# Gate and up of both feed-forward blocks from seven half-size products, with pieces of the down projection between them

## The chip, the cores and the metric

One Trainium2 chip; the kernel runs on one of its cores. The metric is the device time of one execution in microseconds (us), from the first to the last instruction on that core with what the runtime puts around it; less is better. TensorE (PE) does the matmuls, VectorE (DVE), ScalarE (ACT) and GpSimd (POOL) the elementwise work, and one queue, SP, issues all transfers (DMA).

## The reference, cut to what matters

A two-layer decoder trunk over 512 tokens of 1024 features in float32: an attention mixer, an output projection and a SwiGLU feed-forward block (FFN) in each layer. The change concerns the two FFNs:

```python
D_MODEL, SEQ, DEPTH, D_FF = 1024, 512, 2, 2816
for i in range(DEPTH):
    xn = rmsnorm(h, norm_mix[i])
    ...                                     # attention mixer and output projection
    hn = rmsnorm(h, norm_ffn[i])
    h = h + (jax.nn.silu(hn @ ffn_gate[i]) * (hn @ ffn_up[i])) @ ffn_down[i]
return rmsnorm(h, norm_final)
```

## The kernel before

The residual stream `res` stays in on-chip memory (SBUF) as four tiles of 128 tokens. Every float32 operand of a matmul is split into two: `hi`, the value rounded to the matmul's input format, which ACT writes, and `lo`, the rest, which DVE writes (`split`, L213). `mm3` (L266) then makes one product of three matmuls: hi by hi, hi by lo, lo by hi. Weights come in by DMA to a raw tile (`rawb`) and go through `split` into `whi` and `wlo` pieces of 128x1024.

An FFN (`ffn`, L592) runs over 11 units; a unit (the variable `c`) is 256 of the 2816 hidden columns, so two tiles of 128 columns (`m`). For each of the two tiles gate and up are each one accumulation over the 1024 features in a bank of PSUM named `f`: 8 blocks of features (`k`) times `mm3`, the weights stationary and all 512 tokens moving. A unit is so 2 x 2 x 8 x 3 = 96 matmuls of 512 columns. Only unit 0 moves the tokens in two halves of 256, so that it can start before the last token tiles are normalized: 192 matmuls of 256 columns. ACT applies SiLU, DVE multiplies by up, and the hidden tile is split into `hh` and `hl`. After 3, 6, 9 and 11 units a part of the down projection follows (matmuls into banks `s`, L267 to L269; added to `res` at L667, in the last part at L646). Each FFN has 528 matmuls of 512 columns for down. An FFN starts while the output projection before it ends: `norm_steps` normalizes a token tile (DVE one half of its columns, POOL the other), `to_T` transposes it on PE and splits it into `fh` and `fl`.

In the first FFN two other pieces of work lie between: `mem_kv1` (keys and values of the memory for layer 1; two tiles normalized, 16 transposes, 192 matmuls of 256 columns, its hidden operand named `mt`), after the first part; and the first projections of layer 1 (`in_proj`), with the last part.

A scheduler orders the instructions of each engine ahead of time; on the chip each engine takes its own list in that order and waits on semaphores. A tile of a pool has a tag and a number of buffers: the next tile of the same tag waits until the oldest one's readers are done. `WBF` is the number of `whi` and of `wlo` pieces in the FFN.

Of the kernel before, what the change touches and what calls it, by code (L numbers as in the profile page):

```python
# [28 lines left out]
WBF = 4  # L29
# [19 lines left out]
PF = ("sst","","","ooft","ooft")  # L49
LAG = 3  # L50
# [46 lines left out]
def tile_trunk(ctx: ExitStack, tc: tile.TileContext, A, out):  # L97
# [35 lines left out]
    # ---------------------------------------------------------------- constants  # L133
# [10 lines left out]
    # ---------------------------------------------------------------- PSUM tiles: one bank each in the mixers  # L144
# [29 lines left out]
    def norm_steps(g, np_, use, by_pool, use_half=None):  # L174
        """(after the first half of the columns of a token tile, after the second half)"""
# [95 lines left out]
    def proj_T(xh, xl, nk, W, n, evac, N=512, tag="f", eng=split, where=None):  # L271
        """psum[cols 128, N] for each 128 columns of W [nk*128, n]"""
# [10 lines left out]
    def proj_tok(xh, xl, nk, load, n, evac, step, nt=NT, tag="f"):  # L283
        """psum[tokens 128, n] for each token tile, the weights [nk, 128, n] kept for all of them"""
# [14 lines left out]
    def stack_hl(p, scale, dsts):  # L299
        """p psum [128, N] of two heads -> per head [hi; lo] (even) and [lo; hi] (odd)"""  # L300
# [6 lines left out]
    def dup_hl(p, hi, lo):  # L307
        """p psum [64, ...] -> hi, lo on both halves of the partitions"""
# [4 lines left out]
    # ---------------------------------------------------------------- relative bias rows  # L313
# [34 lines left out]
    # ---------------------------------------------------------------- memory attention  # L348
    def mem_kv(i, xm, rs, wk, kv, slot, f32=False, where=None):
# [14 lines left out]
        proj_T(mt[:, 0], mt[:, 1], KD, W[:, 0:256], 256, ek, N=MEML, eng=ENG[MWK[i][0]], where=where)  # L364
# [9 lines left out]
        proj_tok(mt[:, 0], mt[:, 1], KD, rows(W[:, 256:512], where, ENG[MWK[i][1]]), 256, ev, 4, nt=2)  # L374
# [958 lines left out]
```

## Time and profile before

| | before |
|---|---|
| device time, median of 3 runs | 1343.83 us (1343.61 to 1344.03) |
| span of the profiled execution | 1342.6 us |
| PE busy with matmuls | 1272.7 us, 95% |
| DVE, ACT, POOL busy | 724.5, 551.3, 285.6 us (54%, 41%, 21%) |
| mean granted TensorE clock | 0.985 |
| moved by DMA | 126.77 MB, mean 94 GB/s |

The profile is of one execution, and no time of its own stands in it beside its span; it is 1.2 us below the median of the runs. A group row of the profile reads: line, engine, operation, written tile <- read tiles, shapes, count | busy us, mean ns of one | idle time of the engine just before them, and what ended it. A matmul's duration overlaps the next one's, so the distance of two matmuls in a full stream is read from a window: its length over the number of matmuls in it. PEclk is the granted TensorE clock as a share of full speed. The first FFN lies at about 317 to 715 us, the second at about 953 to 1337 us.

### The profile page before, as it was taken

How to read it: one execution, taken by the hardware profiler on the slowest of the kernel's cores; microseconds unless marked ns; L12 is line 12 of the kernel's file. 1: busy time of each engine (PE TensorE's matmuls, PEld its weight loads, DVE VectorE, ACT ScalarE, POOL GpSimd, SP SyncE). 2: the span in 40 equal slices, each digit the busy share in tenths (PEclk: the TensorE clock that was granted, in tenths of full speed). 3: DMA queues.
4: the chain of work that ended last, by engine and by line, in shares of the span. 5: the costliest groups of instructions: out<-in, count | busy, mean ns of one | idle time of the engine just before them, and what ended most of it. 6: DMA issues, size and time to landing. Idle time of an engine off the chain costs nothing.

```text
span 1342.6 us, 17159 instructions
## 1 busy us (share of the span) xinstructions
PE 1272.7 (95%) x6370; PEld 1041.5 (78%) x6370; DVE 724.5 (54%) x1435; ACT 551.3 (41%) x1146; POOL 285.6 (21%) x442
## 2 busy tenths in 40 slices
PE   5989999999999999999999878999899999999997
PEld 5768889798878888888877655678788888888885
DVE  6475778987334333333445899769633333433325
ACT  6375557775322221221334465556432222222231
POOL 6440445635010000000005165552500000000001
PEclk9999999999999999999999989999899999999998
DMA  7742311223224322322321011324221321321311
GB/s 246 215 139 86 110 41 56 69 74 111 95 94 156 113 76 94 109 75 99 103 94 52 22 61 30 94 77 130 79 94 63 126 94 63 125 94 63 126 63 63
DMA packets 107703, 126.77 MB, mean 94 GB/s; under 512 B 5176, under 2 KB 82008, under 8 KB 107620
## 3 DMA queue, kind: packets, MB, share of 16 engines
q1 hardware_dynamic: 107620, 125.68, 28.8%
q8 instruction: 50, 0.82, 0.3%
q14 instruction: 33, 0.27, 0.1%
HBM read 122.22 MB, written 6.58 MB: 96 GB/s over the span
## 4 chain that ended last, share of the span: by engine, by line
PE 61%; DVE 5%; ACT 2%; POOL 2%; issue 1%; DMA 0%; POOLq 0%; DVEq 0%; ACTq 0%
PE f L267 13%; PE f L268 12%; PE f L269 12%; PE s L268 6%; PE s L269 6%; PE s L267 6%; PE o L532 1%; DVE sco L1131 1%; DVE m L1130 1%; PE t L416 1%; DVE sco L1060 1%; POOL xn L204 1%; PE o L464 0%; DVE sb L511 0%; POOL xn L205 0%
## 5 line engine op out<-in xcount | busy, mean ns | idle before, releaser
L214 ACT CAST whi<-rawb 128x1024 fp32r<-128x1024 f32 (+1 forms) x130 | 135.5, 1048 | 461.4 <-PE f L268 276.7
L267 PE MATMUL f<-fh,whi 128*128 128x512 f32 (+1 forms) x768 | 290.5, 380 | 1.9 <-ACT whi L214 1.2
L268 PE MATMUL f<-fl,whi 128*128 128x512 f32 (+1 forms) x768 | 290.6, 379 | 0.0
L269 PE MATMUL f<-fh,wlo 128*128 128x512 f32 (+1 forms) x768 | 290.2, 379 | 0.3 <-DVE wlo L215 0.3
L215 DVE TENSOR_TENSOR wlo<-rawb,whi 128x1024 fp32r<-128x1024 f32 (+1 forms) x130 | 161.1, 1241 | 220.9 <-ACT whi L214 216.9
L267 PEld LDWEIGHTS f<-fh,whi 128*128 128x128 f32 x768 | 145.8, 191 | 31.9 <-ACT whi L214 1.6
L269 PEld LDWEIGHTS f<-fh,wlo 128*128 128x128 f32 x768 | 145.8, 190 | 30.1 <-DVE wlo L215 0.7
L268 PEld LDWEIGHTS f<-fl,whi 128*128 128x128 f32 x768 | 145.8, 190 | 29.3
L183 POOL TENSOR_SCALAR ss<-ss 128x1 f32<-128x1 f32 x16 | 5.6, 350 | 689.2 <-ACT sq L181 689.2
L612 DVE TENSOR_TENSOR sg<-f,sg 128x512 f32<-128x512 f32 x44 | 30.4, 692 | 177.5 <-PE f L269 176.2
L268 PE MATMUL s<-wlo,hh 128*128 128x512 f32 x288 | 115.0, 399 | 0.0
L267 PE MATMUL s<-whi,hh 128*128 128x512 f32 x288 | 112.3, 394 | 0.0
L269 PE MATMUL s<-whi,hl 128*128 128x512 f32 x288 | 111.6, 390 | 0.0
L521 POOL TENSOR_SCALAR sb<-sb,sm 128x128 f32<-128x128 f32 (+3 forms) x144 | 76.6, 548 | 94.5 <-DVE sm L1218 44.7
L517 ACT ACTIVATE sb<-sb,mx 128x128 f32<-128x128 f32 (+3 forms) x144 | 79.5, 555 | 33.7 <-DVE mx L514 33.0
L511 DVE CUSTOM_DVE_ANT_0 sb<-s,M 128x512 f32<-128x512 f32 (+3 forms) x144 | 66.2, 483 | 13.8 <-PE t L416 4.6
L667 DVE TENSOR_TENSOR res<-s,res 128x512 f32<-128x512 f32 x48 | 32.9, 689 | 60.1 <-PE s L269 60.0
L267 PEld LDWEIGHTS s<-whi,hh 128*128 128x128 f32 x288 | 53.9, 187 | 14.2
L269 PEld LDWEIGHTS s<-whi,hl 128*128 128x128 f32 x288 | 54.1, 188 | 12.8
L268 PEld LDWEIGHTS s<-wlo,hh 128*128 128x128 f32 x288 | 54.0, 188 | 12.0
L215 DVE TENSOR_TENSOR ptl<-t,pth 128x512 fp32r<-128x512 f32 (+1 forms) x98 | 57.6, 603 | 4.7 <-ACT pth L214 3.7
L214 ACT CAST pth<-t 128x512 fp32r<-128x512 f32 (+1 forms) x98 | 48.8, 521 | 22.8 <-PE t L392 19.5
(363 smaller groups left out, 2495.4 us busy)
## 6 DMA issues: line engine op xcount, KB each, us to landing
rawb<-in_ffn_gate_dram SPq DMA_DIRECT2D x22, 1024.0 KB, 5.0
rawb<-in_ffn_up_dram SPq DMA_DIRECT2D x22, 1024.0 KB, 5.5
rawb<-in_ffn_down_dram SPq DMA_DIRECT2D x16, 1024.0 KB, 4.9
M<-relskew SPq DMA_DIRECT2D x36, 256.0 KB, 2.7
raw<-in_w_out_dram SPq DMA_DIRECT2D x16, 512.0 KB, 3.5
raw<-in_nsa_w_in_dram SPq DMA_DIRECT2D x12, 512.0 KB, 4.5
rawb<-in_ffn_down_dram SPq DMA_DIRECT2D x12, 512.0 KB, 3.4
relskew<-relrow SPq DMA_DIRECT2D x1, 3072.0 KB
```

The source lines that it names most:

```text
L204: pool.tensor_scalar(dst[:, c], src[:, c], r, 0.0, op0=OP.mult, op1=OP.add)
L214: act.copy(hi, src)
L215: dve.tensor_sub(lo, src, f(hi))
L267: pe.matmul(o, ah, bh, start=start, stop=False)
L268: pe.matmul(o, ah, bl, start=False, stop=False)
L269: pe.matmul(o, al, bh, start=False, stop=stop)
L416: pe.transpose(p[:, j * 128:(j + 1) * 128], b, ident)
L511: dve.tensor_tensor_reduce(E[j, br].rearrange("p (k n) -> p k n", n=128), sv[:, :, x, :], Mi.rearrange("p (k n) -> p k n", n=128), 1.0, -3 ...
L517: act.activation(E[j, br], E[j, br], AF.Exp, bias=mx[:, j, br:br + 1], accum_out=sm[:, j, br:br + 1])
L521: pool.tensor_scalar(E[j, br], E[j, br], fc[:, j, br:br + 1], 0.0, op0=OP.mult, op1=OP.add)
L612: dve.tensor_mul(sg, pp[1], sg)
L667: dve.tensor_add(res[t][:, cs], acc[t], res[t][:, cs])
```

## The change

Unit 0 stays as it was in its matmuls (`gu_plain`). For units 1 to 10 the four products of blocks that a unit consists of (two column tiles by two halves of the features, times two halves of the features by two halves of the tokens) are made by Strassen and Winograd's scheme with seven block products in the place of eight. A block product (`prod`) does gate and up of one block: 2 x 4 x 3 = 24 matmuls with 256 moving columns. The scheme needs sums of weight blocks (four 128x1024 sums for each unit, DVE, in place on the raw tiles `rq` and in `S`), sums of the activations (once for an FFN: `sums`, whose results `T1` to `T4` lie beside the blocks `B11` to `B22` in the buffers `fh`, `fl`, `xh`, `xl`), and sums of the results, which are read out of PSUM between products (`c11`, `c12`, `c22`). Bank `X` keeps accumulating through products 1, 3, 5 and 7 of a unit, bank `Z` holds products 2, and then 4 and 6. Each of the seven weight blocks is split into `whi` and `wlo` (seven splits for a unit in the place of four; `WBF` goes from 4 to 3).

The down projection is cut into pieces of one token tile and half of the output columns (`down_mm`, 12 matmuls, 6 in units 1 and 2); the pieces of the units before stand between the products of the unit at hand, after products 2, 4, 6 and 7 (`CHUNK`). Its weights go through one raw tile (`draw`) and one pair of split tiles (`dhi` in the slot of the block `B12`, which only unit 0 and `sums` read, and `dlo`); one half of the columns of two units' hidden rows at a time. `mem_kv1` now stands in front of unit 2 and uses the `rq` slots for its raw weights. Raw weights come as 8 transfers of 256 KB for a unit (rows of 512 bytes) in the place of 2 of 1 MB (rows of 1 KB). At the start of an FFN ACT copies every transposed piece once more, in float32, for `sums`.

```diff
-WBF = 4
+WBF = 3
+CHUNK = (2, 5, 3, 4)
+RQ = 6
-PF = ("sst","","","ooft","ooft")
+PF = ("sst","","","t","t","o","f")
...
+    def x_halves(fp):
+        fh, fl, th, tl = [big.tile([128, 4, 4, 256], F32R, name=nm("X" + n), tag=n) for n in ("fh", "fl", "xh", "xl")]
+        X = dict(B11=fh[:, 0:2], B21=fh[:, 2:4], B22=fl[:, 0:2], B12=fl[:, 2:4], T1=th[:, 0:2], T3=th[:, 2:4],
+                 T2=tl[:, 0:2], T4=tl[:, 2:4])
+        X["dhi"] = fl[:, 2:4].rearrange("p a k q -> p (a k q)")
...
+                split(pv, X[n][:, 0, :, q], X[n][:, 1, :, q])
+                act.copy(F_[n][:, :, q], pv)
+        def sums():
+            f11, f12, f21, f22 = [F_[n] for n in ("B11", "B12", "B21", "B22")]
+            dve.tensor_sub(f11, f11, f12)
+            dve.tensor_sub(f12, f22, f12)
+            dve.scalar_tensor_tensor(f22, f11, -1.0, f22, op0=OP.mult, op1=OP.subtract)
+            split(f22, X["T2"][:, 0], X["T2"][:, 1])
+            split(f11, X["T1"][:, 0], X["T1"][:, 1])
+            dve.scalar_tensor_tensor(f21, f22, -1.0, f21, op0=OP.mult, op1=OP.subtract)
+            split(f12, X["T3"][:, 0], X["T3"][:, 1])
+            split(f21, X["T4"][:, 0], X["T4"][:, 1])
...
+    def prod(o, w, x, first):
+        xh, xl = x[:, 0], x[:, 1]
+        for m in range(2):
+            oc = o[:, m * 256:(m + 1) * 256]
+            for k in range(4):
+                a, b = w[0][:, m, k], w[1][:, m, k]
+                pe.matmul(oc, a, xh[:, k], start=first and m == 0 and k == 0, stop=False, skip_group_check=True)
+                pe.matmul(oc, a, xl[:, k], start=False, stop=False, skip_group_check=True)
+                pe.matmul(oc, b, xh[:, k], start=False, stop=m == 1 and k == 3, skip_group_check=True)
+    def hid(m, half, o, d, sign, hh, hl):
+        act.activation(d[:, G], o[:, G], AF.Silu, scale=sign)
...
+        split(d[:, U], hh[:, q], hl[:, q])
+    def gu_unit(fp, R, X, hh, hl):
+        A11, A12, A21, A22 = R
+        xb = bank("X")
+        prod(xb, piece(A11), X["B11"], True)
+        c11 = ctile(fp, "c11")
+        act.copy(c11, xb)
+        yield 1
+        z = bank("Z")
+        prod(z, piece(A12), X["B21"], True)
+        dve.tensor_add(c11, z, c11)
+        hid(0, 0, c11, c11, 1.0, hh, hl)
+        yield 2
+        s1 = fp.tile([128, 2, 4, 128], F32, name=nm("S"), tag="S", bufs=1)
+        dve.tensor_add(s1, A21, A22)
+        dve.tensor_add(A21, A11, A21)
+        dve.tensor_add(A11, s1, A11)
+        prod(xb, piece(A11), X["T2"], False)
+        c12 = ctile(fp, "c12")
+        act.copy(c12, xb)
+        yield 6
+        z = bank("Z")
+        prod(z, piece(s1), X["T1"], True)
+        c22 = ctile(fp, "c22")
+        act.copy(c22, z)
+        dve.tensor_add(A12, A11, A12)
+        yield 5
+        prod(xb, piece(A21), X["T3"], False)
+        dve.tensor_add(c22, xb, c22)
+        hid(1, 1, c22, c22, -1.0, hh, hl)
+        yield 7
+        prod(z, piece(A12), X["B22"], False)
+        dve.tensor_add(c12, z, c12)
+        hid(0, 1, c12, c12, 1.0, hh, hl)
+        yield 3
+        prod(xb, piece(A22), X["T4"], False)
+        hid(1, 0, xb, ctile(fp, "c21"), -1.0, hh, hl)
+        yield 4
...
+    def ffn(i, fp, gu0, X, res, fin, early=None, other=None, mt=None):
+        parts = [(0, 1), (1, 3), (3, 5), (5, 7), (7, 9), (9, 11)]
...
+            chunks = down_chunks(i, fp, a, b, half, [hs[k] for k in range(a, b)], X, res)
+            for step in gu_unit(fp, R, X, *hs[c]):
+                if step == 1 or step in CHUNK:
+                    next(chunks)
+            drain(chunks)
```

The order of DVE in the middle of the second FFN, before (here `sg` is the product of SiLU and up, `wlo` and `hl` the low halves of weights and of hidden tiles):

```order
L215 TENSOR_TENSOR wlo_1940_10161<-rawb_1938_10158,whi_1939_10160 128x1024
L612 TENSOR_TENSOR sg_1932_10096<-f_1931_10071,sg_1932_10096 128x512
L215 TENSOR_TENSOR wlo_1942_10165<-rawb_1938_10158,whi_1941_10164 128x1024
L215 TENSOR_TENSOR hl_1933_10099<-sg_1932_10096,hh_1929_10045 128x512
L215 TENSOR_TENSOR wlo_1945_10171<-rawb_1943_10168,whi_1944_10170 128x1024
L612 TENSOR_TENSOR sg_1936_10152<-f_1935_10127,sg_1936_10152 128x512
L215 TENSOR_TENSOR wlo_1947_10175<-rawb_1943_10168,whi_1946_10174 128x1024
L215 TENSOR_TENSOR hl_1937_10155<-sg_1936_10152,hh_1929_10045 128x512
```

And now, from the end of one unit into the next (`rq` is a raw weight block, `c11` to `c21` are results being put together, `hh` the hidden low half, `dlo` the low half of the down weights):

```order
L740 TENSOR_TENSOR rq_2107_12107<-rq_2106_12104,rq_2107_12107 128x1024
L246 TENSOR_TENSOR hh_2071_11796<-c12_2089_11927,hh_2070_11795 128x256
L246 TENSOR_TENSOR wlo_2122_12207<-rq_2106_12104,whi_2121_12206 128x1024
L700 SCALAR_TENSOR_TENSOR c21_2102_12083<-X_2076_11809,c21_2102_12083 128x256
L246 TENSOR_TENSOR dlo_2114_12147<-draw_2115_12148,Xfl_1858_10153 128x1024
L772 TENSOR_TENSOR res_76<-s_2103_12088,res_76 128x512
L246 TENSOR_TENSOR dlo_2114_12147<-draw_2115_12148,Xfl_1858_10153 128x1024
L246 TENSOR_TENSOR hh_2071_11796<-c21_2102_12083,hh_2070_11795 128x256
L246 TENSOR_TENSOR wlo_2126_12238<-S_2120_12202,whi_2125_12237 128x1024
L725 TENSOR_TENSOR c11_2113_12145<-Z_2116_12154,c11_2113_12145 128x512
L246 TENSOR_TENSOR wlo_2130_12283<-rq_2108_12110,whi_2129_12282 128x1024
```

A unit had 4 `wlo`, 2 `sg` and 2 `hl` there, with the down projection's work apart; it now has 28 instructions of DVE, among them 7 `wlo`, 4 sums of weights, 2 `dlo` and 4 additions to `res`, and the two `dlo` stand behind the last product's work (`c21`) and around the addition to `res` of the last piece.

The order of DVE at the end of the second FFN's gate and up, before (`f` is the bank of the last products, `rawb` now holds down weights):

```order
L215 TENSOR_TENSOR hl_2095_11281<-sg_2094_11278,hh_2091_11227 128x512
L612 TENSOR_TENSOR sg_2098_11334<-f_2097_11309,sg_2098_11334 128x512
L215 TENSOR_TENSOR hl_2099_11337<-sg_2098_11334,hh_2091_11227 128x512
L215 TENSOR_TENSOR hl_2102_11343<-rawb_2100_11340,hh_2101_11342 128x512
L215 TENSOR_TENSOR hl_2103_11346<-rawb_2100_11340,hh_2101_11342 128x512
L215 TENSOR_TENSOR hl_2105_11350<-rawb_2100_11340,hh_2104_11349 128x512
```

And now:

```order
L246 TENSOR_TENSOR hh_2241_13331<-c12_2259_13462,hh_2240_13330 128x256
L772 TENSOR_TENSOR res_76<-s_2269_13576,res_76 128x512
L700 SCALAR_TENSOR_TENSOR c21_2272_13618<-X_2246_13344,c21_2272_13618 128x256
L246 TENSOR_TENSOR hh_2241_13331<-c21_2272_13618,hh_2240_13330 128x256
L246 TENSOR_TENSOR dlo_2279_13647<-draw_2280_13648,Xfl_1858_10153 128x1024
L772 TENSOR_TENSOR res_76<-s_2273_13623,res_76 128x512
L246 TENSOR_TENSOR dlo_2279_13647<-draw_2280_13648,Xfl_1858_10153 128x1024
L772 TENSOR_TENSOR res_76<-s_2281_13654,res_76 128x512
```

Before, the low halves of the first down weights (`hl<-rawb`) stood behind the last hidden tile; now a piece of an earlier down projection (`s_2273`) lies between the last product (`X`) and the last down projection (`s_2281`), whose first weights are split further up.

The order of PE where `mem_kv1` starts in the first FFN, before (`mt1` holds the transposed memory, `whi_873` to `whi_881` weight pieces of the memory's keys and values):

```order
L221 MATMUL x_867_4510<-ident_63,xn_866_4507 128x128 x4
L221 MATMUL x_868_4517<-ident_63,xn_866_4507 128x128 x4
L221 MATMUL x_870_4527<-ident_63,xn_869_4524 128x128 x4
L221 MATMUL x_871_4534<-ident_63,xn_869_4524 128x128 x4
L267 MATMUL f_875_4547<-mt1_4493,whi_873_4543 128x256
L267 MATMUL f_887_4657<-whi_881_4621,mt1_4493 128x256
L268 MATMUL f_887_4657<-wlo_882_4622,mt1_4493 128x256
L267 MATMUL f_879_4586<-mt1_4493,whi_877_4582 128x256
L268 MATMUL f_875_4547<-mt1_4493,whi_873_4543 128x256
L269 MATMUL f_875_4547<-mt1_4493,wlo_874_4544 128x256
```

And now (`hh_814`, `hh_816` hold the transposed memory, `rq_877` the second memory tile, `s` are pieces of the down projection of unit 0):

```order
L301 MATMUL s_928_4979<-Xfl_757_3800,hh_818_4022 128x512
L302 MATMUL s_928_4979<-dlo_909_4792,hh_818_4022 128x512
L303 MATMUL s_928_4979<-Xfl_757_3800,hh_819_4023 128x512
L252 MATMUL x_888_4609<-ident_63,rq_877_4567 128x128 x4
L301 MATMUL f_892_4622<-hh_814_4018,whi_890_4618 128x256
L302 MATMUL f_892_4622<-hh_816_4020,whi_890_4618 128x256
L301 MATMUL s_932_5020<-Xfl_757_3800,hh_818_4022 128x512
L302 MATMUL s_932_5020<-dlo_909_4792,hh_818_4022 128x512
L303 MATMUL s_932_5020<-Xfl_757_3800,hh_819_4023 128x512
```

The transposes and products of the memory stood in a block of their own behind unit 2's gate and up; they now stand among the down pieces of unit 0, between the products of units 1 and 2, and their weights pass through the `rq` slots and the three `whi` and `wlo` buffers that the units use.

More of the change, by code (lines that the diff above doesn't have):

```diff
@@ L116, in weights, with hslots, hslot, __init__ @@
         WP.update(es=es, w=wb, r=rb, p=es.enter_context(tc.tile_pool(name=nm("wp"), bufs=1, side="right", reuse_waits="tile")))
-    def hidden():
-        WP["n"] = WP.get("n", 0) + 1
-        return WP["h"].tile([128, 2, 512], F32R, name=nm("hh"), tag=("raw", "whi", "wlo")[WP["n"] % 3], bufs=2)
+    HS = {}
+    def hslots(fp, order):
+        HS.update(fp=fp, order=order, n=0)
+    def hslot(dt=F32R):
+        tag = HS["order"][HS["n"] % len(HS["order"])]
+        HS["n"] += 1
+        where = HS["fp"] if tag == "hx" else WP["h"]
+        return where.tile([128, 1024], dt, name=nm("hh"), tag=tag, bufs=2)
+    class Two:
+        def __init__(self, a, b):
+            self.t = a, b
+        def __getitem__(self, at):
+            p, k, n = at
+            if isinstance(k, slice):
+                return self.t[k.start // 4][p, 0:k.stop - k.start, n]
+            return self.t[k // 4][p, k % 4, n]
+    class Lent:
+        def __init__(self, own, lent):
+            self.own, self.lent = own, lent
+        def tile(self, shape, dt, name=None, tag=None, bufs=1):
+            if tag in self.lent:
+                where, tag, bufs = self.lent[tag]
+                return where.tile(shape, dt, name=name, tag=tag, bufs=bufs)
+            return self.own.tile(shape, dt, name=name, tag=tag, bufs=bufs)
     def nm(s):
@@ new lines, in gu_load, with piece @@
+    def gu_load(i, fp, c):
+        R = []
+        for m in range(2):
+            for j in range(2):
+                r = rq(fp).rearrange("p (m k c) -> p m k c", m=2, k=4)
+                for g, n in enumerate(("ffn_gate", "ffn_up")):
+                    dma(r[:, g], A[n][i][j * 512:(j + 1) * 512, c * 256 + m * 128:c * 256 + m * 128 + 128]
+                        .rearrange("(k p) c -> p k c", p=128))
+                R.append(r)
+        return R
+    def piece(src, pair=None):
+        hi, lo = pair or [WP["p"].tile([128, 1024], F32R, name=nm(x), tag=x, bufs=WP["w"]) for x in ("whi", "wlo")]
+        hi, lo = [x.rearrange("p (m k c) -> p m k c", m=2, k=4) for x in (hi, lo)]
+        split(src, hi, lo)
+        return hi, lo
@@ new lines, in down_mm, with halves_of, down_chunks @@
+    def down_mm(t, half, ks, hh, hl, res):
+        s, cs = slice(t * 128, (t + 1) * 128), slice(half * 512, (half + 1) * 512)
+        p = bank("s")
+        for k, (wh, wl) in enumerate(ks):
+            mm3(p, hh[k][:, s], hl[k][:, s], wh, wl, k == 0, k == len(ks) - 1)
+        dve.tensor_add(res[t][:, cs], p, res[t][:, cs])
+    def halves_of(x):
+        return [x[:, j * 1024:(j + 1) * 1024] for j in range(2)]
+    def down_chunks(i, fp, a, b, half, hs, X, res):
+        ks = down_w(i, fp, a, b, half, halves_of(X["dhi"]), halves_of(dtile(fp, "dlo", F32R)))
+        yield
+        hh, hl = tiles_of(hs)
+        for t in (2, 3, 0, 1):
+            down_mm(t, half, ks, hh, hl, res)
+            yield
@@ new lines, in ffn @@
+    def ffn(i, fp, gu0, X, res, fin, early=None, other=None, mt=None):
+        parts = [(0, 1), (1, 3), (3, 5), (5, 7), (7, 9), (9, 11)]
+        part_of = {c: pi for pi, (a, b) in enumerate(parts) for c in range(a, b)}
+        hs = {}
+        for c in range(parts[-1][1]):
+            hs[c] = hslot(), hslot()
+            R = gu_load(i, fp, c) if c else gu0[0]
+            if c == 0:
+                drain(gu_plain(fp, R, X, *hs[c]))
+                X["sums"]()
+                continue
+            if c == 2 and other:
+                other()
+            pi = part_of[c]
+            a, b = parts[pi - 1] if pi > 1 else parts[0]
+            half = c - parts[pi][0]
+            chunks = down_chunks(i, fp, a, b, half, [hs[k] for k in range(a, b)], X, res)
[3 more added lines that the diff above has]
+            drain(chunks)
+        a, b = parts[-1]
+        both = [down_w(i, fp, a, b, 0, *[[rq(fp, F32R) for _ in range(2)] for _ in range(2)]),
+                down_w(i, fp, a, b, 1, halves_of(X["dhi"]), halves_of(dtile(fp, "dlo", F32R)))]
+        hh, hl = tiles_of([hs[c] for c in range(a, b)])
+        pre, after = fin()
+        each = early(fp) if early else lambda t: None
+        for t in range(NT):
+            for half in range(2):
+                down_mm(t, half, both[half], hh, hl, res)
+                (after if half else pre)(t)
+            if t >= LAG:
+                each(t - LAG)
+        for t in range(NT - LAG, NT):
+            each(t)
```

212 lines of the change are left out of this document (98 added, 114 removed).

## The prediction

> **What bounds the kernel now.** I read the totals and the chain first, then windows of the FFNs, then the groups of each shape.
>
> ```profile
> span 1342.6 us, 17159 instructions
> PE 1272.7 (95%) x6370; PEld 1041.5 (78%) x6370; DVE 724.5 (54%) x1435; ACT 551.3 (41%) x1146; POOL 285.6 (21%) x442
> PE 61%; DVE 5%; ACT 2%; POOL 2%; issue 1%; DMA 0%; POOLq 0%; DVEq 0%; ACTq 0%
> 430.00:560.00 130.00, 130.00 (x557) 104.57 (x556) 46.13 (x50) 33.10 (x39) 0.00 (x0) 1.00 0.30 100
> 966.00:980.00 14.00, 14.00 (x120) 14.00 (x119) 5.05 (x7) 6.05 (x8) 0.00 (x0) 1.00 0.18 56
> 978.74 0.28 PE L268 MATMUL f<-fl,whi 128*128 128x256 f32 x1
> ...
> 982.89 0.28 PE L267 MATMUL f<-fh,whi 128*128 128x256 f32 x1
> L268 PE MATMUL f<-fl,whi 128*128 128x512 f32 x640 | 253.8, 396 | 0.0
> L268 PE MATMUL f<-fl,whi 128*128 128x256 f32 x128 | 36.8, 292 | 0.0
> L268 PEld LDWEIGHTS f<-fl,whi 128*128 128x128 f32 x768 | 145.8, 190 | 29.3
> ```
>
> The chain that ended last is matmuls; no other engine has over 5% of it. Behind the length of a window stand PE, PEld, DVE, ACT and POOL, then clock, DMA share and GB/s. From 430 to 560 us, all 512-column matmuls, PE is never idle at the full clock, DVE is busy for 35% of the time, ACT for 25%: this stage is bound by the matmuls' number and length alone. Spacing: 130/557 = 0.2334 us. From 966 to 980 us PE runs unit 0, 256 columns each: 14/120 = 0.1167. A window also counts the matmuls cut by its edges; from the start at 978.74 to the one at 982.89 there are 35 steps in the timeline, 0.1186 each. I take 0.118. So half the columns cost 0.505 of the time, though each matmul has its own weight load of 190 ns in both shapes: the loads overlap.
>
> **The change part by part.** *Products.* For each of 20 units (10 for each FFN) 96 x 0.2334 = 22.4 us are removed, 7 x 24 = 168 x 0.118 = 19.8 us added: -2.58, so **-51.7 us**. Unit 0 and the 528 down matmuls of an FFN keep number and shape. All of it was on the path. With 0.1167 it would be -56, with 0.120 it would be -45: these are the ends.
>
> *Cover in a steady unit.* PE now needs 19.8 + 4 pieces x 12 x 0.2334 (11.2) = 31.0 us.
>
> ```profile
> L215 DVE TENSOR_TENSOR wlo<-rawb,whi 128x1024 fp32r<-128x1024 f32 x55 | 67.4, 1225 | 102.1 <-ACT whi L214 100.1
> L667 DVE TENSOR_TENSOR res<-s,res 128x512 f32<-128x512 f32 x24 | 16.5, 689 | 30.8 <-PE s L269 30.8
> L215 DVE TENSOR_TENSOR cat<-o,cat 128x256 fp32r<-128x256 f32 x10 | 4.2, 417 | 2.4 <-ACT cat L214 2.4
> L214 ACT CAST whi<-rawb 128x1024 fp32r<-128x1024 f32 x55 | 57.8, 1051 | 225.7 <-PE f L268 136.8 <-PE s L269 69.0 <-DMA rawb<-in_ffn_gate_dram 16.0
> L214 ACT CAST fh<-x 128x512 fp32r<-128x512 f32 x16 | 9.2, 586 | 19.6 <-PE x L221 19.6
> L214 ACT CAST cat<-o 128x256 fp32r<-128x256 f32 x10 | 3.8, 376 | 4.0 <-PE o L464 2.5 <-PE o L532 1.5
> raw<-in_w_out_dram SPq DMA_DIRECT2D x16, 512.0 KB, 3.5
> raw<-in_nsa_w_in_dram SPq DMA_DIRECT2D x12, 512.0 KB, 4.5
> ```
>
> DVE's 28 instructions: 13 of 1024 elements (7 `wlo`, 2 `dlo`, 4 sums, which also read two SBUF tiles) x 1.225 = 15.9; 4 additions to `res` and 3 of results x 0.69 = 4.8; 8 of 256 x 0.417 = 3.3; together 24.1 us, 78% of PE's 31.0. ACT: 9 casts x 1.051, 3 copies x 0.586, 8 of 256 x 0.376 = 14.2 us, 46%. Both lie beside PE, but with far less room than DVE's 35% now. A product and a piece (2.83 + 2.80 = 5.6 us) stand between one use of bank `X` or `Z` and the next; the copy or addition that must come between takes 0.59 or 0.69.
>
> The tightest chain is the single pair of down weights, released by the last piece of a unit. From the end of product 7: PE goes on with piece 4 (2.80), products 1 and 2 (2.83 each), and wants the new down weights at 8.46. DVE by its list: `wlo` behind ACT's cast to 2.44 (0.16 + 1.05 + 1.23; 0.16 is what the 396 ns of a matmul exceed the spacing by), `c21` to 2.86; ACT's cast of `dhi` from 2.96 (piece 4 and 0.16) to 4.01; `dlo` to 5.24, `res` to 5.93, the second `dlo` to 7.15. The first half has 3.2 us to spare; the second, wanted six matmuls later at 9.86, has 2.7. So the steady unit costs nothing more, except that an in-order queue at 78% is now and then one `wlo` late: between 0 and 0.5 us for each unit, nearest to the 0.0 idle of the matmul rows above, I take 0.15: **+3 us** (0 to 10).
>
> *Transfers.* The two rows of 512 KB differ in packet length (`w_out` 2 KB, `nsa_w_in` 512 bytes): 1.0 us more, so 256 KB about 0.5 more each. A unit moves 3 MB in 31 us, about what it did in 33.6 us at a share of 0.30; 8 + 1 issues of about 3 us each, with six `rq` slots for four blocks, so half a unit ahead (15 us). Cost 0. If that cover were gone, 4 x 3 us for each unit would show; SP's list is in order, so one late slot holds all behind it.
>
> *Start of an FFN.*
>
> ```profile
> 940.00:960.00 20.00, 14.91 (x71) 11.91 (x70) 15.66 (x23) 12.40 (x27) 16.24 (x20) 0.88 0.32 106
> ```
>
> ACT copies 8 pieces more (0.586 each). Unit 0's first products want token tiles 0 and 1, so one or two copies stand in front of a cast that PE waits for; the rest lies beside 22.6 us of unit 0. 0 to 4.7 us, taken 1.2, since POOL, 16.24 of 20 us busy at the second start, sets the pace there: **+2.4** for both. `sums` (4 sums and 4 low halves, 8 x 1.225 = 9.8 us of DVE) has until product 3 of unit 1, and DVE has 9 of 14 us free in the second window above: 0.
>
> *`mem_kv1`.* It is now mixed into units 1 and 2 of the first FFN.
>
> ```profile
> 393.67 0.38 PE L267 MATMUL f<-mt,whi 128*128 128x256 f32 x1 [1.13 <-ACT mt L214]
> 395.28 0.39 PE L267 MATMUL f<-mt,whi 128*128 128x256 f32 x1 [0.99 <-DVE mt L215]
> L231 POOL TENSOR_TENSOR wlo<-rawb,whi 128x1024 fp32r<-128x1024 f32 x2 | 4.8, 2380 | 60.4 <-ACT whi L230 57.2 <-PE x L221 3.2
> 390.00:430.00 40.00, 37.66 (x209) 32.63 (x208) 17.98 (x24) 13.20 (x22) 2.35 (x1) 0.96 0.40 137
> ```
>
> Now it costs PE 2.3 us of idle time in 40 us. Its four weight pieces were split far ahead (DVE 45% busy); now their raw tiles wait for `rq` slots and their splits stand among the units' own. Late by a full split (1.05 + 1.23 us) each, and two by POOL's 2.38 more, it is 4 x 2.28 + 4.8 = 14 us; split ahead it is -2.3, since the present waits go. I take the middle: **+5**.
>
> *End of gate and up.* Before, PE waits there for the last hidden tile:
>
> ```profile
> 1309.78 0.69 DVE L612 TENSOR_TENSOR sg<-f,sg 128x512 f32<-128x512 f32 x1 [9.18 <-PE f L269]
> 1312.51 0.50 PE L268 MATMUL s<-hl,hh 128*128 128x512 f32 x1 [1.91 <-DVE hl L215]
> L268 PE MATMUL s<-hl,hh 128*128 128x512 f32 x64 | 25.8, 408 | 3.4 <-DVE hl L215 3.4
> 1280.00:1320.00 40.00, 38.09 (x157) 30.27 (x156) 12.33 (x18) 10.21 (x17) 0.00 (x0) 0.96 0.14 51
> ```
>
> Now 12 matmuls (2.8 us) lie behind the last product, and its work (0.38 + 0.42 + 0.38 + 0.42 = 1.6 us) fits under them: **-3.4** for both FFNs. Bounds -3.4 and 0.
>
> *The clock.* After the 1.91 us gap the clock of the 40 us window is 0.96, so 1.6 us lost. The start of the first FFN shows the same:
>
> ```profile
> 317.51 0.39 PE L267 MATMUL f<-fh,whi 128*128 128x256 f32 x1 [0.74 <-ACT whi L214]
> 318.46 0.39 PE L267 MATMUL f<-fh,whi 128*128 128x256 f32 x1 [0.42 <-ACT whi L214]
> 323.06 0.41 PE L268 MATMUL f<-fl,whi 128*128 128x256 f32 x1
> 323.27 0.41 PE L269 MATMUL f<-fh,wlo 128*128 128x256 f32 x1
> 324.16 0.28 PE L267 MATMUL f<-fh,whi 128*128 128x256 f32 x1
> 324.28 0.28 PE L268 MATMUL f<-fl,whi 128*128 128x256 f32 x1
> 320.00:324.00 4.00, 3.59 (x17) 3.23 (x18) 4.00 (x5) 4.00 (x9) 3.55 (x5) 0.57 0.28 90
> ```
>
> Gaps of 0.74 and 0.42 us, and matmuls 0.21 us apart until 324, then 0.12 (the clock of 320 to 324 is 0.57). So short gaps close together cost about 1.6 us more. I count -1.6 for the end of the second FFN and +1.6 for `mem_kv1`: **0**. The Trainium skill, TensorE: Matmul & The Clock Gate, section "Why this matters for your kernels", asks only for "No PE-idle gaps >~3µs between matmul bursts". By it both terms would be nothing and the sum the same; the trace does not agree, its gaps of 1.91 and 0.74 us are followed by the lower clock.
>
> Sum: -51.7 + 3 + 0 + 2.4 + 5 - 3.4 + 0 = -44.7, so 1342.6 - 44.7 = 1297.9 for the span; the median of the runs lies 1.2 above it: **1299 us**. The bounds that I think may meet: products -54 to -48, units 0 to 8, start 1 to 4, `mem_kv1` 0 to 9, end -3.4: about 1288 to 1313. 0.2% (2.7 us) is what a measurement can tell from no change.
>
> **The rivals.** *Small gaps lower the clock.* If half of the units had gaps of 0.8 us in front of a product and lost 1.6 us to the clock each time, 10 x 2.4 = +24: 1323. For it: DVE's load and the rows at 317 us. Against: in the steady unit no wait ends within 2.7 us of being late. By the rule of the Trainium skill given above such gaps would cost themselves alone, 8 us, and 1307.
>
> *Down weights too late: slower.* Place: the chain behind product 7. If it ended 2.7 us later than reckoned, every further us costs 20; at 2.7 + 44.7/20 = 4.9 us late the gain is gone, and 6 us late gives 1299 + 3.3 x 20 = 1365. It takes four to five more `wlo` in front of `dlo`. Against: DVE's list has none there.
>
> *Half-size matmuls cost more than half.* At the 0.190 us of a weight load a unit takes 168 x 0.19 = 31.9 and not 19.8: +242, 1541; at 96 x 0.2334/168 = 0.133 the change saves nothing (1343). The Trainium skill, TensorE: Matmul & The Clock Gate, section "Back-to-back issue gap", has streams of loads and matmuls at 81 ns for 128 and 131 for 512 columns; an estimate between them, 98 for 256, would make a unit 16.4 us in the place of 12.6, +77 in all. The rows at 430 and 966 us settle this against it: 0.2334 and 0.1167 to 0.118.
>
> **How the numbers follow.** The forecast, 1288 to 1313, has 0.72; clock and waits, 1313 to 1338, 0.17; slower by the down weights 0.04, by the half-size matmuls 0.01; near 1343 0.02; better than 1288, with `mem_kv1` hidden and no waits, 0.04. Range: the forecast and the nearer half of the first rival, 1288 to 1323, holds 0.80. Faster 0.72 + 0.17 + 0.04 = 0.93, within 0.2% 0.02, slower 0.05.
>
> **What would show it.** Right: a window in the middle of either FFN with PE never idle, some 216 matmuls in 31 us, DVE near 78%, clock 1.00; no wait for a hidden low half at the end of gate and up; both FFNs shorter, the second by some 26 us, the first by less, with its idle time at `mem_kv1`. Wrong: waits of products for `wlo` or of pieces for `dlo` in every unit, PEclk under 1 there, or matmuls of 256 columns further apart than 0.12 us.

## The result, and the profile after

The changed kernel takes **1299.31 us** (median of 4 runs, 1290.12 to 1301.25) against 1343.93 us of the kernel before (4 runs, 1343.61 to 1345.70): ratio 0.9655, 95% interval 0.9622 to 0.9688, so faster. The forecast was 1299. The profiled execution has a span of 1299.5 us and a mean granted clock of 0.975 (before 0.985).

The totals of the page of the changed kernel:

```profile
span 1299.5 us, 20995 instructions
PE 1219.0 (94%) x7810; PEld 1079.4 (83%) x7810; DVE 967.7 (74%) x1763; ACT 672.4 (52%) x1370; POOL 284.6 (22%) x442
```

PE is still the bound, with 1440 more matmuls that are shorter (7810 against 6370) and 53.7 us less of busy time; DVE has 243 us more work. Windows of 40 us from the middle of the second FFN (columns as in the prediction):

```profile
1080.00:1120.00 40.00, 40.00 (x286) 37.43 (x285) 29.60 (x37) 18.95 (x27) 0.00 (x0) 1.00 0.34 100
1120.00:1160.00 40.00, 40.00 (x282) 37.26 (x281) 28.49 (x36) 17.55 (x26) 0.00 (x0) 1.00 0.36 112
```

PE is never idle and has the full clock, DVE is busy for 71 to 74% of the time, ACT for 44 to 47%: the steady unit stands as forecast. Three groups of it, which answer to the `f` groups of before:

```profile
L688 PE MATMUL X<-Xxl,whi 128*128 128x256 f32 x320 | 89.6, 280 | 0.0
L690 PE MATMUL X<-Xfh,wlo 128*128 128x256 f32 x208 | 59.4, 286 | 2.0 <-DVE wlo L246 2.0
L302 PE MATMUL s<-dlo,hh 128*128 128x512 f32 x320 | 125.9, 393 | 1.0 <-DVE dlo L246 1.0
```

The idle time behind the bar is one wait each, both at `mem_kv1` (below). To compare stages I take the end of the last residual addition of each output projection and each FFN from the timelines of DVE. The kernel before:

```profile
317.52 0.68 DVE L569 TENSOR_TENSOR res<-f,res 128x512 f32<-128x512 f32 x1
714.26 0.69 DVE L646 TENSOR_TENSOR res<-s,res 128x512 f32<-128x512 f32 x1 [0.73 <-PE s L269]
953.52 0.68 DVE L569 TENSOR_TENSOR res<-f,res 128x512 f32<-128x512 f32 x1
1335.73 0.69 DVE L646 TENSOR_TENSOR res<-s,res 128x512 f32<-128x512 f32 x1
```

And the changed kernel:

```profile
323.41 0.68 DVE L602 TENSOR_TENSOR res<-f,res 128x512 f32<-128x512 f32 x1
700.62 0.68 DVE L772 TENSOR_TENSOR res<-s,res 128x512 f32<-128x512 f32 x1
941.95 0.67 DVE L602 TENSOR_TENSOR res<-f,res 128x512 f32<-128x512 f32 x1
1291.74 1.28 DVE L772 TENSOR_TENSOR res<-s,res 128x512 f32<-128x512 f32 x2
```

The same four ends were read in every profile of the study (us):

| profile | mixer 0 | FFN 1 | mixer 1 | FFN 2 |
|---|---|---|---|---|
| before, three profiles | 318.2, 321.3, 322.2 | 396.8, 394.2, 396.3 | 239.2, 238.7, 238.6 | 382.2, 382.2, 382.4 |
| changed, two profiles | 324.1, 322.2 | 377.2, 378.0 | 241.3, 240.7 | 350.4, 350.8 |
| difference of the means | +2.6 | -18.2 | +2.2 | -31.7 |
| eight plain products | 317.7 | 402.1 | 242.1 | 378.0 |
| before, 256 columns | 321.6 | 400.0 | 238.9 | 384.2 |
| pieces written behind product 7 | 319.5 | 377.8 | 239.4 | 352.1 |
| every second `wlo` twice | 323.0 | 378.7 | 241.8 | 350.2 |
| every `wlo` twice | 321.1 | 391.9 | 242.1 | 361.9 |
| changed, no `mem_kv1` | 319.5 | 354.1 | 238.8 | 350.5 |
| before, no `mem_kv1` | 318.9 | 379.7 | 241.0 | 381.7 |
| DVE normalizes | 324.1 | 373.8 | 240.7 | 347.2 |
| DVE normalizes, pieces behind | 323.8 | 370.5 | 241.1 | 349.0 |

The two FFNs gave 49.9 us, and the mixers took 4.8 of it back. (In the first pair of profiles alone the mixers took 8.0.) The change leaves the attention of the mixers alone, but not their edges: the transposes at the end of the output projection stand elsewhere, and the weights of layer 1's first projections go through other tiles.

An FFN's length mixes its start with its units. So I also cut at the first of the last eight residual additions of each output projection, and at the first product of unit 1 (the 193rd matmul of gate and up, in order of time). "Start" lies between these two, "units" from there to the end of the FFN, and "mixer" is the rest:

| profile | mixer 0 | start 1 | units of FFN 1 | mixer 1 | start 2 | units of FFN 2 |
|---|---|---|---|---|---|---|
| before, three profiles | 305.7, 308.8, 309.6 | 40.0, 38.9, 39.7 | 369.3, 367.8, 369.1 | 224.5, 224.0, 223.8 | 44.5, 44.5, 44.7 | 352.5, 352.5, 352.5 |
| changed, two profiles | 313.7, 311.8 | 43.1, 43.7 | 344.6, 344.7 | 226.5, 225.9 | 43.5, 43.9 | 321.7, 321.6 |
| difference of the means | +4.7 | +3.8 | -24.2 | +2.1 | -0.9 | -30.8 |
| eight plain products | 307.3 | 43.5 | 369.0 | 228.8 | 41.3 | 350.0 |
| changed, no `mem_kv1` | 309.8 | 41.5 | 322.3 | 224.0 | 43.6 | 321.7 |
| before, no `mem_kv1` | 306.4 | 40.6 | 351.6 | 226.3 | 43.9 | 352.5 |
| DVE normalizes | 311.0 | 41.9 | 345.1 | 225.1 | 40.9 | 321.9 |

### The profile page after: what moved, and what is told of

The parts are those of the page before. It is cut to its first block, busy times and chain, and to the rows that moved or that the text cites. A ratio compares the mean times of both kernels' runs of the same rounds, so it can differ in the third digit from the quotient of the medians.

```text
span 1299.5 us, 20995 instructions
## 1 busy us (share of the span) xinstructions
PE 1219.0 (94%) x7810; PEld 1079.4 (83%) x7810; DVE 967.7 (74%) x1763; ACT 672.4 (52%) x1370; POOL 284.6 (22%) x442
## 5 line engine op out<-in xcount | busy, mean ns | idle before, releaser
L245 ACT CAST whi<-rq 128x1024 fp32r<-128x1024 f32 x128 | 134.3, 1051 | 212.2 <-issue 121.7
L246 DVE TENSOR_TENSOR wlo<-rq,whi 128x1024 fp32r<-128x1024 f32 x128 | 159.1, 1251 | 39.9 <-ACT whi L245 39.8
L302 PE MATMUL s<-dlo,hh 128*128 128x512 f32 x320 | 125.9, 393 | 1.0 <-DVE dlo L246 1.0
L303 PE MATMUL s<-Xfl,hh 128*128 128x512 f32 x320 | 126.3, 395 | 0.0
L301 PE MATMUL s<-Xfl,hh 128*128 128x512 f32 x320 | 124.4, 394 | 0.0
L688 PE MATMUL X<-Xxl,whi 128*128 128x256 f32 x320 | 89.6, 280 | 0.0
L690 PE MATMUL X<-Xxl,wlo 128*128 128x256 f32 x320 | 89.6, 280 | 0.0
L689 PE MATMUL X<-Xxl,whi 128*128 128x256 f32 x320 | 89.5, 280 | 0.0
L303 PEld LDWEIGHTS s<-Xfl,hh 128*128 128x128 f32 x320 | 60.0, 188 | 13.3
L302 PEld LDWEIGHTS s<-dlo,hh 128*128 128x128 f32 x320 | 60.1, 188 | 12.4 <-DVE dlo L246 1.3
L301 PEld LDWEIGHTS s<-Xfl,hh 128*128 128x128 f32 x320 | 60.0, 188 | 11.0 <-DVE res L772 0.3
L689 PEld LDWEIGHTS X<-Xxl,whi 128*128 128x128 f32 x320 | 60.1, 188 | 1.8
L688 PEld LDWEIGHTS X<-Xxl,whi 128*128 128x128 f32 x320 | 60.2, 188 | 1.7
L690 PE MATMUL X<-Xfh,wlo 128*128 128x256 f32 x208 | 59.4, 286 | 2.0 <-DVE wlo L246 2.0
L245 ACT CAST pth<-t 128x512 fp32r<-128x512 f32 (+1 forms) x98 | 48.9, 521 | 23.5 <-PE t L425 20.3
```

The source lines that it names most:

```text
L245: act.copy(hi, src)
L246: dve.tensor_sub(lo, src, f(hi))
L301: pe.matmul(o, ah, bh, start=start, stop=False)
L302: pe.matmul(o, ah, bl, start=False, stop=False)
L303: pe.matmul(o, al, bh, start=False, stop=stop)
L688: pe.matmul(oc, a, xh[:, k], start=first and m == 0 and k == 0, stop=False, skip_group_check=True)
```

## The experiments

**The changed kernel once more**, nothing edited.

> The changed kernel once more, nothing edited. In its first profile the mixer of layer 0, whose instructions stand in the same order as before, took 8.0 us longer (313.69 against 305.67 us to its end), with matmuls at half the clock around 83 to 92 and 141 to 153 us. Theory: that is how transfers and the clock fall out in one execution, and not the change; then the mixer's length differs here by several us from the 313.7, and the median lies between 1288 and 1301. Rival: the change itself moves the mixer's end (other places in memory, another layout); then the mixer takes 313 to 315 us again in this profile.

1299.53 us (4 runs, 1296.31 to 1299.74); ratio 0.9659 (0.9641 to 0.9678). By the expectation's marker (the first of the last eight residual additions) the mixer took 311.8 us, 1.9 less than the first time: outside the rival's 313 to 315, but too little to settle it, so it was taken up again with the kernel before (last experiment).

**Eight plain products in the place of seven.** The sums go; the pieces stay between the products.

```diff
-        A11, A12, A21, A22 = R
-        xb = bank("X")
-        prod(xb, piece(A11), X["B11"], True)
...
-        prod(xb, piece(A22), X["T4"], False)
+        for m in range(2):
+            w = [piece(R[2 * m + j]) for j in range(2)]
+            for half in range(2):
+                o = bank("X")
+                for j in range(2):
+                    prod(o, w[j], X[f"B{j + 1}{half + 1}"], j == 0)
+                hid(m, half, o, ctile(fp, ("c11", "c21")[half]), 1.0, hh, hl)
...
```

> The changed kernel with eight plain products of 24 matmuls in each of units 1 to 10 in the place of seven: no sums of weights, activations or results; the pieces of the down projection still stand between the products. Theory (the gain is the missing eighth product, 24 x 0.117 us for each of 20 units): +56 us on the changed kernel, 1350 to 1358, so slower than before by some 10 us. Rival (the gain is the placing of the pieces and the way the FFN is staged): 1295 to 1310. In between, 1310 to 1340, if the sums cost part of the gain.

1350.65 us (5 runs); against before 1.0046 (1.0030 to 1.0061). The missing product is the gain: with eight products the kernel is 51 us slower than the changed one, and its units are 24.4 us (FFN 1) and 28.3 us (FFN 2) longer, where 240 matmuls x 0.117 = 28.1 each were to be expected. So the sums and the three more splits cost nothing in the units of FFN 2. The 3.7 us that are short in FFN 1 most likely belong to `mem_kv1`: without it the changed kernel's units take as long in FFN 1 as in FFN 2 (322.3 and 321.7). The new staging by itself is worth nothing over the whole kernel (FFN 1 +6.3, FFN 2 -4.3 against the kernel before).

**256 columns in the kernel before.**

```diff
-                        first = c == 0
+                        first = True
```

> The kernel before with the gate and up products of every unit in two halves of 256 columns, as its unit 0 has them: 20 x 96 more matmuls and weight loads, the same number of columns. Theory (a matmul of 256 columns stands 0.117 us from the next, 0.501 of the 0.2334 of 512): 1344 to 1348. By the 0.118 that the prediction took, 20 x 192 x 0.0013 = +5 us: 1349. Rival (the weight load of 190 ns sets the distance): 20 x 192 x 0.073 = +280 us: 1624.

1352.48 us, 1.0056 (1.0039 to 1.0073): +7.6 us for 1920 matmuls of 512 columns cut in two, so 0.0040 us for each, 0.1187 for a half. The rival, a weight load of 190 ns as the distance, is out. A window of it:

```profile
1200.00:1240.00 40.00, 40.00 (x339) 40.00 (x339) 12.46 (x13) 10.91 (x14) 0.00 (x0) 1.00 0.29 93
```

339 matmuls in 40 us, 0.118, and PEld, second, is now busy for the whole 40 us. In the changed kernel PEld is at 37.4 of 40, and the starts of its product 7 (1263.02 to 1265.84 us for 24 matmuls) stand 0.1175 apart. That the loads are what spaces a pure stream of 256 columns out a little is suggested by this, and not shown.

**All pieces behind product 7**, in the order in which the program writes them.

```diff
-CHUNK = (2, 5, 3, 4)
+CHUNK = ()
```

> The changed kernel with all four pieces of the down projection behind product 7 of a unit, none between the products. Theory (the pieces between are the cover of DVE's work): the seven products then take 19.7 us, in which DVE has 7 wlo, 4 sums, 3 results and 4 hidden pieces, 7 x 1.23 + 4 x 1.23 + 3 x 0.69 + 4 x 0.8 = 18.8 us, 95%, with three buffers of wlo ahead; late splits of 1 to 3 us for each unit, so +20 to +60 us: 1320 to 1360. Rival (only the average load of DVE, 75% of a unit, counts, and the buffers carry it over): 1297 to 1305.

1297.12 us, 0.9643 (0.9619 to 0.9667): the rival's number, and the window from 1080 to 1120 us again has PE at 40.00 and DVE at 28.09. But the experiment does not test what its expectation says. The scheduler orders PE's list, and it moved about half of the pieces forward again. PE's matmuls into `s` in one unit, first from the unit's start to the end of product 7, then behind it; the changed kernel first, then this one:

```profile
1084.20:1111.60 27.40, 8.78 (x36) 1.00 0.38 115
1111.60:1114.40 2.80, 2.71 (x12) 1.00 0.00 0
```

```profile
1110.30:1134.90 24.60, 5.81 (x23) 1.00 0.36 108
1134.90:1140.70 5.80, 5.74 (x25) 1.00 0.28 81
```

(Behind the window and its length: PE busy with these matmuls and their number, clock, DMA share, GB/s.) So 13 of 48 matmuls moved, and not 36. That this costs nothing is shown; a unit with no piece between its products was not run, and my theory about it stays open.

**Low halves computed twice**, every second one, and every one (7 x 1.23 = 8.6 us more of DVE for a unit).

```diff
         split(src, hi, lo)
+        if pair is None:
+            dve.tensor_sub(lo, src, f(hi))
```

> The changed kernel with every second low half of a gate and up weight block computed twice by DVE: 3.5 x 1.23 = 4.3 us of DVE more for each of 20 units of 30.9 us. DVE's 73% of a unit becomes 87%. Theory (only the average load of DVE counts, the buffers carry single late halves, as with all pieces behind the products): 1299 to 1306, no PE waits in the middle of an FFN. Rival (the first rival of the prediction: a fuller DVE makes small gaps, and they lower the clock): half of the units with 0.8 us of gap and 1.6 us of clock, +24 us: 1323.

> The changed kernel with every low half of a gate and up weight block computed twice: 7 x 1.23 = 8.6 us of DVE more for a unit, 22.6 + 8.6 = 31.2 us against the 30.9 us of PE. Theory (only DVE's sum counts): DVE becomes the bound by a little, 0.3 to 2 us for a unit, with gaps in every unit and the clock under 1.00 there: 1305 to 1345. Rival (DVE has no part in the time): 1299.

1303.52 us (0.9698, 0.9669 to 0.9727) and 1324.59 us (0.9852, 0.9835 to 0.9868). Windows of the first and of the second:

```profile
1080.00:1120.00 40.00, 40.00 (x285) 37.38 (x284) 35.43 (x44) 19.05 (x29) 0.00 (x0) 1.00 0.30 91
```

```profile
1080.00:1120.00 40.00, 37.70 (x275) 35.28 (x274) 37.65 (x45) 18.92 (x28) 0.00 (x0) 1.00 0.27 80
1240.00:1280.00 40.00, 40.00 (x275) 36.96 (x274) 38.22 (x47) 15.88 (x25) 0.00 (x0) 1.00 0.17 53
```

With DVE at 89% of the window (up to 93% in one from 980 to 1020 us) PE still never waits, and the FFNs are within 1.1 us of the changed kernel's. At 94% to 96% it begins to wait in some units: +14.3 us in FFN 1, +11.3 in FFN 2, of which 10.6 and 7.4 lie in units 1 to 10 and the rest at the starts, where low halves of unit 0 are doubled too. The clock of these two windows is 1.00 all the same, but a gap at 499 us in FFN 1 was followed by a stretch at half clock (0.50 from 500 to 502 us). The prediction's first rival (small gaps of DVE's making, each with 1.6 us of clock) needs a DVE well above 89% first, and in the changed kernel DVE is busy for 74% from 440 to 680 us and for 75% from 980 to 1250 us.

**No `mem_kv1`**, in the changed kernel and in the kernel before: the memory's keys and values for layer 1 are not computed, rows of the memory are copied in their place.

```diff
...
-            mem_kv(1, xm, rs, ng, kp, mt, True, fp, True)
+            for t in range(2):
+                dma(f(kp[t].rearrange("p a b -> p (a b)")), A["mem"][0, t * 128:(t + 1) * 128])
```

> The changed kernel without the keys and values of the memory for layer 1 (rows of the memory stand in their place, copied by transfers): prices mem_kv1. Theory (its raw weights wait for rq slots, so its products stand late): 16 transposes and 192 matmuls, 1.8 + 22.5 us, 5.9 us of idle PE and 1.6 to 3 us of clock go, so -32 us: 1265 to 1269. Rival (its idle time only moves to another place): -24 us, 1275.

> The kernel before with the same part left out. There it stands in a block of its own with 2.3 us of idle PE and little clock: 1.8 + 22.5 + 2.3 + 1 = 27.6 us less, 1315 to 1318. If both prices are the same, the change's step of +5 us for mem_kv1 was not there; by the waits it should be +3.6 to +5.

1272.35 us and 1332.93 us: 27.2 us less than the changed kernel, 11.2 less than the one before. My count of 192 matmuls, here and in the words on the kernel before, was wrong: 192 is both layers' memory, `mem_kv1` alone has 96, so 11.2 us and not 22.5. Its price by the length of FFN 1 is 16.1 us before (1.8 + 11.2 + 2.3 of waits = 15.3 foreseen with the right count) and 23.5 after, so 7.4 dearer; but the starts differ between these profiles too. By the units of FFN 1 alone it is 17.2 us before and 22.3 after: the change made it 5.2 us dearer, which answers to the prediction's +5. The totals differ by more, 16 us, since they hold the mixers, which vary.

**DVE normalizes both halves of a token tile**, alone and with the pieces written behind product 7.

```diff
-NSP = (0,1)
+NSP = (0,0)
```

> The changed kernel with DVE normalizing both halves of a token tile's columns at the starts of the FFNs (and of layer 1's norm), where POOL had the second half (1.22 + 2.12 or 0.69 + 1.65 us against 0.73 on DVE). Theory (the starts wait for POOL: 1.24 + 3.77 us in front of the second FFN): 2 to 5 us less, one or two half-clock windows of 3.41 us fewer there: 1293 to 1298. Rival (DVE, 82 to 92% busy at the starts, is late in its place: the waits of 2.21 and 1.59 us for its own xn at the first FFN grow by 0.7 each): 1299 to 1304.

> The same, and with all four pieces of the down projection behind product 7. As the placing of the pieces was worth nothing by itself (1297.1 against 1299.5), the same times as for DVE's normalizing alone, 1292 to 1298 by the theory that the starts wait for POOL; 1297 to 1304 by the rival.

1292.49 us, 0.9604 (0.9583 to 0.9626), and 1293.62 us, 0.9615 (0.9592 to 0.9638). The waits of 1.24 and 3.77 us for POOL at the start of FFN 2 become one of 2.55 us for DVE, one window of 3.41 us at half clock is gone there, and start 2 is 2.8 us shorter: at FFN 2 the theory holds. Start 1 is 1.5 us shorter, but its waits before were mostly for DVE and ACT, so POOL's part there is not shown (most of the 3.8 us by which FFN 1 is shorter in the first table is a later end of mixer 0). The first of the two has the lowest median of the study that still computes all; one of the eight runs of the changed kernel, 1290.12 us, was as short.

**The kernel before once more**, twice, for layer 0's mixer alone.

> The kernel before once more, nothing edited, for the length of layer 0's mixer, whose instructions stand in the same order in all kernels here. So far its end (last residual addition of the output projection) was at 317.5 us in the kernel before and 316.9 to 323.4 us in the others, with 3.4 to 12 us lost to half-clock windows. Theory (the windows of 3.41 us fall at another phase in every execution, and the mixer's length with them): an end anywhere from 317 to 323 us, 3.4 to 10 us of clock loss. Rival (the changed kernel's layer 0 is slower for a reason of its own): an end at 317 to 319 us, 3 to 5 us of clock loss, as in its first profile.

> The same again: by the theory another length and another phase, anywhere from 317 to 323 us; by the rival 317 to 319 us.

1344.40 and 1347.42 us, one run each. The last addition starts at 320.6 and 321.5 us (317.5 the first time), and 6.8 and 8.5 us were lost to half clock in that mixer (3.4 the first time). The profile that I predicted from had a lucky mixer: the same instructions vary by some 4 us from one execution to the next. By the marker of the first experiment the three profiles of the kernel before stand at 305.7, 308.8 and 309.6 us, and the seven of kernels with the new FFN in which POOL still normalizes at 307.3 to 313.7. The ranges overlap, but the changed kernel's own two, 313.7 and 311.8, lie above all three of before; that its layer 0 is a little slower for a reason of its own is not excluded.

## Why the prediction was right, and where its steps were not

The number and the direction were right, and the mechanism was: eight plain products put the time back to that of before. The sum, step by step, by the lengths of the stages:

- *Products, -51.7 forecast: about -55.* FFN 2 from its first product of unit 1 (971.30 us) to the down piece behind its last product (1265.84 us) is 294.5 us for 1680 matmuls of 256 columns and 420 of 512; with 0.2334 for the latter that leaves 0.1170 for the former, not 0.118, so 20 x (22.4 - 19.66). This term was mis-sized, within its ends (-56 to -45). The row from which I took 0.118 was of a pure stream of 256 columns, which the experiment on the kernel before confirms for such a stream (0.118 to 0.1187). The units of FFN 2 agree: 30.8 us shorter, of which 1.9 of gap and 1.7 of clock lay at their end.
- *Steady units, +3 forecast: 0.* From 440 to 700 us and from 965 to 1290 us no PE wait is listed. DVE turned out to carry 89% without one.
- *Transfers, 0 forecast: 0 in the steady units.* The share of the DMA engines is 0.34 and 0.36 in the two windows above, 0.30 before, and PE waits for nothing there.
- *Start of an FFN, +2.4 forecast: about +3*, not even: some +4 at the first, -1 at the second. The size is right, but the mechanism, a copy of ACT in front of a cast, is at most a part of what the rows show. At the first the waits for normalized tiles grew, and the time at half clock (6.8 us against 3.4; in the other profiles 10.2 against 0 and 3.4):

```profile
324.93 0.63 PE L644 MATMUL x<-ident,xn 128*128 128x128 f32 x4 [2.21 <-DVE xn L238]
327.56 0.59 PE L688 MATMUL X<-Xfh,whi 128*128 128x256 f32 x2 [0.94 <-ACT Xfh L245]
329.75 0.66 PE L644 MATMUL x<-ident,xn 128*128 128x128 f32 x2 [1.59 <-DVE xn L238]
```

- *`mem_kv1`, +5 forecast: +5.2* by the units of FFN 1, by the mechanism named, raw weights late behind the `rq` slots. PE's waits there (5.9 us in all, against 2.3 before), ACT's casts that wait for the transfers, and what the queue SP waited for from 360 to 410 us before it could issue the memory's weights (L297) and the next unit's (L671); the numbers there are us in all, times, and the longest:

```profile
385.30 0.50 PE L302 MATMUL s<-dlo,hh 128*128 128x512 f32 x1 [0.97 <-DVE dlo L246]
395.06 0.38 PE L301 MATMUL f<-hh,whi 128*128 128x256 f32 x1 [1.84 <-ACT whi L245]
396.32 0.58 PE L303 MATMUL f<-hh,wlo 128*128 128x256 f32 x1 [0.76 <-DVE wlo L246]
404.38 0.38 PE L690 MATMUL X<-Xfh,wlo 128*128 128x256 f32 x1 [1.97 <-DVE wlo L246]
```

```profile
393.96 1.05 ACT L245 CAST whi<-rq 128x1024 fp32r<-128x1024 f32 x1 [0.44 <-DMA rq<-in_w_mem_kv_dram]
396.34 1.05 ACT L261 CAST whi<-rq 128x1024 fp32r<-128x1024 f32 x1 [1.33 <-DMA rq<-in_w_mem_kv_dram]
```

```profile
SPq L671 <- POOL wlo L262: 5.5, 2, 3.1
SPq L297 <- PE x L252: 3.9, 2, 2.6
SPq L297 <- DVE wlo L246: 3.4, 2, 2.3
```

- *End of gate and up, -3.4 forecast: -3.4.* The last product runs into the down piece, and no wait for a hidden low half is left:

```profile
1265.72 0.28 PE L690 MATMUL X<-Xxl,wlo 128*128 128x256 f32 x1
1265.84 0.39 PE L301 MATMUL s<-Xfl,hh 128*128 128x512 f32 x1
```

- *The clock, 0 forecast: -1.7.* At the end of FFN 2 the 1.7 us went as said. The +1.6 at `mem_kv1` did not come: one half-clock stretch of 3.41 us stands there in both profiles of the changed kernel, and in two of the three of before. What the step left out is the rest of the kernel: the mean clock of the runs is 0.974 to 0.981 (8 runs) where it was 0.978 to 0.986 in the runs of before beside them and beside the other kernels. That is, at most (1 - 0.976) x 1298 = 31 us lost against (1 - 0.983) x 1344 = 23. Most of it lies in the two mixers: 38 and 41 us of them are at half clock in the profiles of the changed kernel, 17 to 27 before.

With the mixers' +6.9 by the second table (foreseen 0; the start is counted from the same marker) the terms give -55 + 0 + 3 + 5.2 - 3.4 - 1.7 + 6.9 = -45, and the stages measured -45.1. So the forecast of -44.7 hit partly by luck, because errors met: the FFNs gave 5 us more than reckoned (49.9 for 44.7), FFN 2 alone 31.7 where "some 26" was written, and the mixers took as much back. What the sum lacked is a term for the mixers.

Their part is not settled. Mixer 0 is within what kernels with the same layer 0 differ by. In mixer 1 a part has a place: 13 to 14 us behind the end of FFN 1 PE waits for the first projections' output, before and now,

```profile
727.71 0.66 PE L1029 MATMUL t<-ident,in1a 128*128 128x128 f32 x4 [1.36 <-DVE in1a L1023]
715.73 0.66 PE L1184 MATMUL t<-ident,in1a 128*128 128x128 f32 x4 [2.69 <-DVE in1a L1178]
```

and the wait is 2.68 to 2.71 us in all nine profiles with the new FFN, each time with a half-clock stretch 14 to 17 us behind the end of FFN 1; it is 1.11 to 2.10 in the five with the old one, and there none comes within 41 us. So the new staging costs something at this seam, with seven products or eight. But the whole of mixer 1 does not follow it: the changed kernel without `mem_kv1` is at 224.0, as before, and the kernel before without it at 226.3.

Of the rivals, the gaps with a lower clock did not come in the steady units, nor the late down weights (no piece waits for `dlo` there), nor the dear half-size matmuls.

## What to carry to other kernels

Where one engine is never idle, count its instructions by their distance in a full stream, taken from a stream of the mixture that will run, and check each other engine by its sum for one round of the loop: here, with three buffers of weight pieces between, PE did not wait with DVE busy for 89% of a window, and did at 94%. The terms that are hard to size are at the seams, where a pipeline starts or foreign work is mixed in, so price those by leaving them out. When an edit is meant to move work, look in the trace whether it moved: here the scheduler undid most of one. And compare stages over several profiles: code that nobody changed differed by 4 us between executions.

## What was not expected of the hardware

**The half clock comes in windows on a fixed grid.** By the traces' records of the granted clock, the half-clock stretches of every profile last 3.41 us or a multiple of it (but for the last, which the end of the execution cuts), and within one execution all begin on one grid of 3.413 us: before, at 320.51, 395.60, 757.41 and 1313.78 us among others, which are 22, 106 and 163 steps apart. Over 14 profiles, from 300 us on, a grid window with 1.8 us or more of idle PE was followed by a window at half clock in 114 cases of 116; with 1.2 to 1.8 us in 27 of 60; with less in 16 of 3965. The clock that the window itself had decides the middle: out of full clock, 1.2 to 1.8 us of idle PE were followed by half clock in 5 of 38 cases and less in none of 3868; out of half clock, 1.2 to 1.8 us in 22 of 22 and less in 16 of 97. So a gap's price depends on where it falls, and less idle time keeps the half clock than brings it about. Windows of 2 us, first of the kernel before at the ends of the two FFNs' gate and up, with gaps of 1.48 and 1.91 us, then of the changed kernel with its gap of 1.97 us that ends at 404.38:

```profile
690.00:692.00 2.00, 0.52 (x3) 0.21 (x2) 1.42 (x3) 0.55 (x1) 0.00 (x0) 1.00 0.00 0
692.00:694.00 2.00, 2.00 (x9) 1.65 (x10) 2.00 (x4) 0.00 (x0) 0.00 (x0) 1.00 0.03 8
...
1310.00:1312.00 2.00, 0.60 (x3) 0.17 (x1) 1.32 (x3) 0.62 (x1) 0.00 (x0) 1.00 0.00 0
1312.00:1314.00 2.00, 1.49 (x6) 1.28 (x7) 2.00 (x4) 0.00 (x0) 0.00 (x0) 0.95 0.00 0
1314.00:1316.00 2.00, 2.00 (x6) 1.52 (x6) 2.00 (x5) 0.00 (x0) 0.00 (x0) 0.50 0.04 8
```

```profile
402.00:404.00 2.00, 0.41 (x4) 0.20 (x2) 2.00 (x1) 0.50 (x2) 1.24 (x1) 1.00 0.49 146
404.00:406.00 2.00, 1.62 (x13) 1.62 (x14) 1.91 (x4) 0.37 (x1) 0.00 (x0) 1.00 0.72 213
406.00:408.00 2.00, 2.00 (x19) 2.00 (x18) 1.33 (x3) 0.54 (x2) 0.00 (x0) 1.00 0.18 53
```

The gap of 1.91 us (1310.6 to 1312.5) lies inside one window of its grid (1310.37 to 1313.78) and is followed by 0.50; the longer one of 1.97 us is cut at 402.94 into 0.5 and 1.44 and costs only itself. The prediction's argument on the clock, which read 1.6 us of loss from single gaps, was right for those gaps and no rule. The Trainium skill, TensorE: Matmul & The Clock Gate, section "Part 1: The HAM clock gate (the "warmup" mystery)", gives a free-running window of 3413 ns; the runs agree on its length and on its not following the kernel. They do not agree that a whole window must be idle: somewhat over half of one is enough.
